# Time mixing: the substitution ahead of the strict scores, the queries behind the merges

## The chip, the cores and the metric

The kernel runs on one core of one Trainium2 chip. The metric is device microseconds (us) of one execution. Five engines work side by side, each through its own queue in a fixed order: TensorE (PE; its weight loads are listed as PEld), VectorE (DVE), ScalarE (ACT), GpSimd (POOL) and SyncE (SP, which only issues transfers here). An instruction that waits holds up everything behind it on its engine.

## The reference

The program runs two small transformer blocks of two layers each over 256 tokens of width 1024. The change lies in the first mixer, a recurrence over tokens with 16 heads of width 64:

```python
def _rwkv7_step(S, inp):
    r, w, k, v, a, b = inp
    sa = jnp.einsum('bhvk,bhk->bhv', S, a)
    S = S * w[:, :, None, :] + sa[..., None] * b[:, :, None, :] + v[..., None] * k[:, :, None, :]
    y = jnp.einsum('bhvk,bhk->bhv', S, r)
    return S, y
...
    y = jnp.moveaxis(y, 0, 1)
    mean = jnp.mean(y, axis=-1, keepdims=True)
    var = jnp.mean(jnp.square(y - mean), axis=-1, keepdims=True)
    yn = ((y - mean) * lax.rsqrt(var + LNX_EPS)).reshape(B, T, D) * lnx_w + lnx_b
    bonus = (jnp.sum(rh * kh * r_k, axis=-1, keepdims=True) * vh).reshape(B, T, D)
    out = ((yn + bonus) * g).astype(x.dtype)
    return out @ w_o
```

Seven more stages follow it (feed-forward, two kinds of attention and more); they take about 1130 of the 1420 us and their code isn't touched.

## The kernel before

**How the recurrence is computed.** It isn't stepped through. Tokens come in two blocks of 128 (b = 0, 1) and heads in two halves of eight (H = 0, 1). Within a block the recurrence is a triangular system for each head, I minus a strictly lower triangular matrix, and its inverse is built up by size: 16x16 blocks, then 32x32, then 64x64.

- `rwkv_base` (L1720 on) makes the small diagonal blocks on PE (L1745), masks them on DVE (L1747), and inverts all 16x16 blocks at once by forward substitution: for each row r from 2 to 15 one product (L1768) and one sum (L1769) on DVE, each needing the one before. Transposes and a copy (L1772 to L1774) put the result where the merges read it.
- `rwkv_strict` (L1839) computes the full 128x128 lower triangular scores for each H and b by `rwkv_scores`: PE at L1848 into a PSUM bank, DVE at L1850 from the bank with the mask. There are four such (H, b), each with two banks.
- `rwkv_merge` (L1783) joins blocks in four rounds of many tiny matmuls, which this text calls r1 to r4: r1 (L1791, 256 matmuls of 32x16) and its copy on DVE (L1792), r2 (L1798) and L1800 to L1804, r3 (L1811, which reads the strict scores) and L1818, r4 (L1824) and L1827. The copies L1827 fill Y64, the inverse of 64x64.
- `rwkv_solve` (L1854) makes the key scores (again L1848 and L1850, with other operands), sums them with the values (L1863), and applies Y64 in two halves (L1879 and its copy L1880, with L1874 and L1876 between). For b = 0 the state update L1887 and L1888 follows.
- `rwkv_gate` (L1917) projects the output gate on PE (L290 to L292 and L1925) and copies it on ACT (L1926). `rwkv_query` (L1928) multiplies the queries (L1934), transposes them on PE (L1702, copied at L1704 and L1705), makes the bonus sums (L1937 to L1940) and the bonus terms on POOL (L1943 to L1947).

The projections of key, value and query (`project`, 48 groups of L290 to L292 for each half of the columns) run in the background: `weave` steps its generators in turn and calls `tick`, which emits one step of the background list. Their weights are cut in two parts by the feeder at L88 (ACT) and L89 (DVE).

**What sets the order.** The code emits instructions in the order in which `weave` steps the generators. A scheduler then sorts each engine's queue, by what is ready in its own model of time and by the numbers given with `pri` or `high_priority`; a higher number goes first. `issue_after(ins)` ties all instructions that the block emits on the engine of `ins` behind `ins` in that engine's queue. PSUM has eight banks in rings: `tp` and `acc` have four each in this stage until L1586, where `tp` and `long` get four each.

Of the kernel before, what the change touches and what calls it, by code (L numbers as in the profile page):

```python
# [16 lines left out]
OP = mybir.AluOpType  # L17
# [131 lines left out]
class K:  # L149
# [1265 lines left out]
    def rwkv(self):  # L1415
        nc, W, A = self.nc, self.W, self.a
# [9 lines left out]
        for i in range(2):  # L1426
            c = slice(64 * i, 64 * i + 64)
# [15 lines left out]
        with self.tc.high_priority(1000):  # L1443
            for b in range(2):
# [4 lines left out]
                for g in range(2):  # L1449
                    p = self.tp()  # L1450
# [27 lines left out]
        raw = {}  # L1478
# [61 lines left out]
        E = [{"mv": self.sm(16, tag="mv", bufs=2)} for _ in range(2)]  # L1540
# [22 lines left out]
        xr = shifted(0, True)  # L1563
        self.bg.append(project("r", xr))
        self.weave([self.pri(1000, self.rwkv_keys(E[H], raw["k"][H])) for H in range(2)], n=1)
        self.weave([self.pri(200, self.rwkv_base(E))] + [self.pri(0, self.rwkv_strict(E[H])) for H in range(2)], n=1)
        while len(self.bg) > 1:
            self.tick()
        W.lo_pool = False
        gate = self.gate_parts(hid)  # L1570
        self.weave([self.pri(1000, self.rwkv_merge(E[H])) for H in range(2)] + [self.pri(400, self.rwkv_gate(H, E[H], *gate)) for H in range(0)], n=2)
        solve = ([self.pri(400, self.rwkv_solve(H, 0, E[H], raw["v"][H])) for H in range(2)]
                 + [self.pri(400, self.rwkv_gate(H, E[H], *gate)) for H in range(0, 2)])
        if 0:
            self.rings(2, 4, 2)
            self.weave(solve, n=0)
            solve = []
        self.drain()
        W.lo_pool = False
        W.cap = W.n_split  # L1580
        self.rings(0, 4, 4)
        vecs = [self.bcast(A[n][0].rearrange("h n -> (h n)") if n == "a_r_k" else A[n][0], D)
                for n in ("a_r_k", "a_lnx_w", "a_lnx_b")]
        self.weave(solve + [self.pri(400, self.rwkv_query(H, E[H], raw, vecs)) for H in range(2)])
        self.rope_setup()
        W.cap = len(W.plan)  # L1586
        W.grow(4)
# [195 lines left out]
    def rwkv_merge(self, E):  # L1783

        nc = self.nc
        Moff, P1z, Xv, Yc, Y32, Y64 = (E[n] for n in ("Moff", "P1z", "Xv", "Yc", "Y32", "Y64"))
        p1 = self.tp()
        for h in range(16):
            for i in range(4):
                s = slice(32 * i, 32 * i + 32)  # L1790
                nc.tensor.matmul(p1[s, h * 16:(h + 1) * 16], Moff[s, h, :], Xv[s, h, :], start=True, stop=True)  # L1791
        nc.vector.tensor_copy(P1z[:, :, :16], p1[:, :256].rearrange("p (h c) -> p h c", h=16))  # L1792
        yield
        pz = self.tp()
        for h in range(16):
            for i in range(4):
                s = slice(32 * i, 32 * i + 32)
                nc.tensor.matmul(pz[s, h * 16:(h + 1) * 16], P1z[s, h, :], Yc[s, h, :], start=True, stop=True)  # L1798
        nc.vector.tensor_scalar(Y32[:, :, :16], Yc, self.even, None, op0=OP.mult)
        nc.vector.scalar_tensor_tensor(Y32[:, :, 16:], Yc, self.odd, pz[:, :256].rearrange("p (h c) -> p h c", h=16),  # L1800
                                       op0=OP.mult, op1=OP.add)
        flat = lambda t: t.rearrange("p h c -> p (h c)")
        X32 = Moff
        nc.vector.transpose(flat(X32), flat(Y32))  # L1804
        yield
        p1 = self.tp()
        for h in range(16):
            b, hd = self.unhb(h)
            for i in (0, 64):
                s, t = slice(i, i + 32), slice(i + 32, i + 64)  # L1810
                nc.tensor.matmul(p1[t, h * 32:(h + 1) * 32], E["SM", b][s, hd, t], X32[s, h, :], start=True, stop=True)  # L1811
        P1 = P1z
        for i in (0, 64):
            s, t = slice(i, i + 32), slice(i + 32, i + 64)
            nc.gpsimd.memset(Y64[t, :, :32], 0.0)
            nc.scalar.activation(Y64[s, :, :32], Y32[s], AF.Copy)
            nc.scalar.activation(Y64[t, :, 32:], Y32[t], AF.Copy)
            nc.vector.tensor_copy(P1[t], p1[t].rearrange("p (h c) -> p h c", h=16))  # L1818
        yield
        pz = self.tp()  # L1820
        for h in range(16):
            for i in (0, 64):
                s, t = slice(i, i + 32), slice(i + 32, i + 64)
                nc.tensor.matmul(pz[s, h * 32:(h + 1) * 32], P1[t, h, :], Y32[t, h, :], start=True, stop=True)  # L1824
        for i in (0, 64):
            s = slice(i, i + 32)
            nc.vector.tensor_copy(Y64[s, :, 32:], pz[s].rearrange("p (h c) -> p h c", h=16))  # L1827
        yield

    @staticmethod  # L1830
# [98 lines left out]
    def rwkv_query(self, H, E, raw, vecs):  # L1929
        nc = self.nc  # L1930
        r_k, lnx_w, lnx_b = (self.vec_half(t, H) for t in vecs)
        heads = lambda t: t.rearrange("p b (h n) -> p (b h) n", h=8)
        R, V, EP = raw["r"][H], raw["v"][H], E["EP"]
        nc.vector.tensor_tensor(EP, R, EP, op=OP.mult)  # L1934
        E["R2"] = []
        yield from self.feat_pairs(EP, E["R2"])
        nc.gpsimd.tensor_tensor(R, E["Kt"], r_k, op=OP.mult)  # L1937
        nc.vector.tensor_tensor(R, EP, R, op=OP.mult)
        bon = self.sm(16)
        nc.vector.tensor_reduce(bon, heads(R), axis=AX.X, op=OP.add)  # L1940
        T2, G = R, E["G"]
        yield
        nc.gpsimd.tensor_tensor(heads(T2), heads(V), self.over_cols(E["mv"], 64), op=OP.add)  # L1943
        nc.gpsimd.tensor_tensor(heads(T2), heads(T2), self.over_cols(bon, 64), op=OP.mult)
        nc.gpsimd.tensor_tensor(T2, T2, lnx_b, op=OP.add)
        nc.gpsimd.tensor_tensor(T2, T2, G, op=OP.mult)
        nc.gpsimd.tensor_tensor(G, G, lnx_w, op=OP.mult)  # L1947
        E["T2"] = T2
# [122 lines left out]
```

## Time and profile before

| | |
|---|---|
| median of 3 runs | 1421.07 us (1416.91 to 1426.39) |
| profiled execution, its own time | 1423.76 us |
| its span | 1421.9 us |
| mean granted TensorE clock | 0.971 |
| busy share of the span: PE, DVE, ACT, POOL | 94%, 69%, 51%, 22% |
| the part of the stage that the change moves | about 94 to 191 us of the span |

The span lies 1.86 us under the execution's own time. A granted clock of 1.00 is 2.4 GHz, of 0.50 is 1.2 GHz. The busy shares are averages over eight stages; what the change is worth is read from its own stretch.

### The profile page before, as it was taken

The page shows a single profiled execution, that of the slowest core. Times are in us where ns is not written, and L with a number is a line of the kernel's source. Part 1 is how long each engine was busy: PE and PEld are TensorE (multiplying, and loading weights), DVE is VectorE, ACT ScalarE, POOL GpSimd, SP SyncE. Part 2 cuts the span into 40 slices and gives each one's busy share as a digit, 9 for nine tenths or more (in the row PEclk, how much of TensorE's full clock was granted, in tenths as well). Part 3 has the DMA queues.
Part 4 walks back from the last instruction along what each step waited for, and adds up shares of the span by engine and source line. Part 5 has one row for each costly group of instructions (what it writes and reads, how often), then busy time and mean ns, then how long its engine had stood idle before and what let it go on. Part 6 is the DMA issues. An engine that isn't in the chain of part 4 may idle for free. (4 is left out here: it accounts for less than half of the span.)

```text
span 1421.9 us, 20925 instructions
## 1 busy us (share of the span) xinstructions
PE 1339.9 (94%) x7819; PEld 1116.4 (79%) x7819; DVE 982.4 (69%) x1712; ACT 723.2 (51%) x1276; POOL 312.1 (22%) x278
## 2 busy tenths in 40 slices
PE   7998799989999799999999999999999998999998
PEld 5786699778888687788877777788888776788887
DVE  7889545788854675678864688677633897687642
ACT  5843212566643575576654555555543545465431
POOL 4201621100000100133222353222322631111110
PEclk9998599999999899999999999999999999999999
DMA  8345002466672452275574544265763632266662
GB/s 259 120 128 181 2 16 80 159 204 183 193 237 89 147 169 60 90 217 183 178 225 150 178 148 119 87 202 185 227 194 96 206 114 80 74 195 191 191 197 87
DMA packets 153574, 214.79 MB, mean 151 GB/s; under 512 B 11700, under 2 KB 95900, under 8 KB 153472
## 3 DMA queue, kind: packets, MB, share of 16 engines
q1 hardware_dynamic: 152608, 210.31, 47.6%
q10 hardware_dynamic: 864, 3.15, 0.6%
q8 instruction: 61, 1.00, 0.3%
q14 instruction: 41, 0.34, 0.1%
HBM read 212.37 MB, written 1.05 MB: 150 GB/s over the span
## 5 line engine op out<-in xcount | busy, mean ns | idle before, releaser
L88 ACT ACTIVATE s_slot<-s_slot 128x1024 fp32r<-128x1024 f32 (+2 forms) x221 | 229.6, 1045 | 166.8 <-PE bank L292 104.6
L89 DVE TENSOR_TENSOR s_slot<-s_slot,s_slot 128x1024 fp32r<-128x1024 f32 (+1 forms) x180 | 224.7, 1254 | 102.7 <-ACT s_slot L88 102.1
L89 DVE TENSOR_TENSOR rwkv_slot<-s_slot,rwkv_slot 128x1024 fp32r<-128x1024 f32 (+4 forms) x121 | 151.8, 1261 | 91.7 <-ACT rwkv_slot L88 91.2
L88 ACT ACTIVATE rwkv_slot<-s_slot 128x1024 fp32r<-128x1024 f32 (+3 forms) x141 | 144.7, 1034 | 88.3 <-PE bank L292 52.3
L89 POOL TENSOR_TENSOR s_slot<-s_slot,s_slot 128x1024 fp32r<-128x1024 f32 x41 | 100.9, 2460 | 303.0 <-ACT s_slot L88 283.0
L532 PE MATMUL bank<-ffn_slot,s_slot 128*128 128x512 f32 x320 | 115.2, 401 | 5.4 <-DVE ffn_slot L537 5.4
L532 PE MATMUL bank<-ffn_slot,rwkv_slot 128*128 128x512 f32 x280 | 98.4, 395 | 0.0
L532 PE MATMUL bank<-mlp_slot,s_slot 128*128 128x512 f32 x272 | 96.7, 396 | 0.6 <-DVE mlp_slot L537 0.6
L266 POOL TENSOR_TENSOR rwkv_sm<-rwkv_sm,mhalf 128x1 f32<-128x1 f32 x32 | 19.8, 618 | 340.0 <-DVE rwkv_sm L263 339.2
L534 PE MATMUL bank<-ffn_slot,s_slot 128*128 128x256 f32 x320 | 89.9, 281 | 0.0
L534 PE MATMUL bank<-ffn_slot,rwkv_slot 128*128 128x256 f32 x280 | 77.8, 278 | 0.0
L532 PEld LDWEIGHTS bank<-ffn_slot,s_slot 128*128 128x128 f32 x320 | 61.2, 191 | 20.8 <-DVE ffn_slot L537 6.4
L534 PE MATMUL bank<-mlp_slot,s_slot 128*128 128x256 f32 x272 | 75.8, 279 | 0.0
L89 POOL TENSOR_TENSOR rwkv_slot<-s_slot,rwkv_slot 128x1024 fp32r<-128x1024 f32 (+1 forms) x20 | 47.3, 2364 | 92.6 <-ACT rwkv_slot L88 75.1
L290 PE MATMUL bank<-s_slot,mlp_slot 128*128 128x512 f32 x160 | 62.6, 391 | 0.1
L292 PE MATMUL bank<-s_slot,mlp_slot 128*128 128x512 f32 x160 | 62.3, 390 | 0.0
L291 PE MATMUL bank<-s_slot,mlp_slot 128*128 128x512 f32 x160 | 62.3, 389 | 0.0
L532 PEld LDWEIGHTS bank<-ffn_slot,rwkv_slot 128*128 128x128 f32 x280 | 52.5, 188 | 12.4 <-DVE ffn_slot L537 0.3
L534 PEld LDWEIGHTS bank<-ffn_slot,s_slot 128*128 128x128 f32 x320 | 61.3, 192 | 0.0
L532 PEld LDWEIGHTS bank<-mlp_slot,s_slot 128*128 128x128 f32 x272 | 51.0, 188 | 12.8 <-DVE mlp_slot L537 0.9
L534 PEld LDWEIGHTS bank<-ffn_slot,rwkv_slot 128*128 128x128 f32 x280 | 52.6, 188 | 0.2
L532 PE MATMUL bank<-mlp_slot,rwkv_slot 128*128 128x512 f32 x144 | 51.7, 398 | 0.6 <-DVE mlp_slot L537 0.6
(514 smaller groups left out, 3549.4 us busy)
## 6 DMA issues: line engine op xcount, KB each, us to landing
s_slot<-in_mlp_w_dram SPq DMA_DIRECT2D x128, 512.0 KB, 4.4
s_slot<-in_ffn_w_in_dram SPq DMA_DIRECT2D x88, 512.0 KB, 4.2
s_slot<-in_ffn_w_out_dram SPq DMA_DIRECT2D x44, 512.0 KB, 4.2
s_slot<-in_a_w_rkv_dram SPq DMA_DIRECT2D x24, 512.0 KB, 4.4
s_slot<-in_diff_w_in_dram SPq DMA_DIRECT2D x32, 256.0 KB, 4.2
s_slot<-in_dsa_w_in_dram SPq DMA_DIRECT2D x16, 512.0 KB, 4.1
s_slot<-in_a_w_o_dram SPq DMA_DIRECT2D x8, 512.0 KB, 3.9
s_slot<-in_o_w_dram SPq DMA_DIRECT2D x8, 512.0 KB, 3.9
```

The lines of the kernel that those rows point to most:

```text
L88: k.nc.scalar.activation(hi, raw, AF.Copy)
L89: (k.nc.gpsimd if low else k.nc.vector).tensor_tensor(lo, raw, hi, op=OP.subtract)
L266: nc.gpsimd.tensor_tensor(r, u, self.mhalf[:, 0:1], op=OP.pow)
L290: mm(out, lh, rh, start=start, stop=False)
L291: mm(out, lh, rl, start=False, stop=False)
L292: mm(out, ll, rh, start=False, stop=stop)
L532: mm(o, wh[:, kt % 4, c], a.rearrange("p c t -> p (c t)"), start=kt == 0, stop=False, skip_group_check=True)
L534: mm(o[:, :T], wl[:, kt % 4, c], a[:, 0], start=False, stop=kt == 7, skip_group_check=True)
```

## The change

The substitution is woven alone, before any strict scores. The merges and the strict scores are then stepped together by hand: twice one step of both merges and two steps of each strict generator, and then the rest. The merges take their banks from the `acc` ring, since the strict scores hold those of `tp`. Solve, gate and query are emitted inside `issue_after` on the merges' last copy (L1827), which is a DVE instruction, so it is their DVE instructions that are tied. One product of the bonus sums (L1937) goes from POOL to DVE.

```diff
-        self.weave([self.pri(200, self.rwkv_base(E))] + [self.pri(0, self.rwkv_strict(E[H])) for H in range(2)], n=1)
+        self.weave([self.pri(1000, self.rwkv_base(E))], n=1)
         while len(self.bg) > 1:
             self.tick()
-        W.lo_pool = False
         gate = self.gate_parts(hid)
-        self.weave([self.pri(1000, self.rwkv_merge(E[H])) for H in range(2)] + [self.pri(400, self.rwkv_gate(H, E[H], *gate)) for H in range(0)], n=2)
-        solve = ([self.pri(400, self.rwkv_solve(H, 0, E[H], raw["v"][H])) for H in range(2)]
-                 + [self.pri(400, self.rwkv_gate(H, E[H], *gate)) for H in range(0, 2)])
...
+        merges = [self.pri(1000, self.rwkv_merge(E[H])) for H in range(2)]
+        strict = [self.pri(300, self.rwkv_strict(E[H])) for H in range(2)]
+        for _ in range(2):
+            for g in (*merges, *strict, *strict):
+                next(g, None)
+            self.tick(2)
+        self.weave([*strict, *merges], n=2)
         self.drain()
...
-        self.weave(solve + [self.pri(400, self.rwkv_query(H, E[H], raw, vecs)) for H in range(2)])
+        with ExitStack() as st:
+            for e in E:
+                st.enter_context(self.tc.issue_after(e["merged"].ins))
+            self.weave([self.pri(400, self.rwkv_solve(H, 0, E[H], raw["v"][H])) for H in range(2)]
+                       + [self.pri(400, self.rwkv_gate(H, E[H], *gate)) for H in range(2)]
+                       + [self.pri(400, self.rwkv_query(H, E[H], raw, vecs)) for H in range(2)])
@@ rwkv_merge
-        p1 = self.tp()
+        p1 = self.acc()
...
-            nc.vector.tensor_copy(Y64[s, :, 32:], pz[s].rearrange("p (h c) -> p h c", h=16))
+            E["merged"] = nc.vector.tensor_copy(Y64[s, :, 32:], pz[s].rearrange("p (h c) -> p h c", h=16))
@@ rwkv_query
-        nc.gpsimd.tensor_tensor(R, E["Kt"], r_k, op=OP.mult)
+        nc.vector.tensor_tensor(R, E["Kt"], r_k, op=OP.mult)
```

The lines of the changed kernel stand 3 higher in this stage: its L1853 is L1850 of before, its L1795 is L1792. The text keeps to the numbers of before.

First, DVE from the last sum of the substitution to the first copy of the merges. Before, the queue holds a key score (bank 67), three instructions of the bonus sums (L1938, L1940) and another key score ahead of the copy L1792:

```order
L1769 TENSOR_REDUCE rwkv_slot_794<-rwkv_slot_796 128x2x15
L1772 STREAM_TRANSPOSE rwkv_slot_796<-rwkv_slot_794 128x512
L1773 COPY rwkv_slot_794<-rwkv_slot_794 128x512
L1774 STREAM_TRANSPOSE rwkv_slot_796<-rwkv_slot_794 128x512
L1799 TENSOR_SCALAR rwkv_slot_1070<-rwkv_slot_796,even_odd 128x16x16 x2
L1850 TENSOR_TENSOR rwkv_slot_1508<-bank_67,rwkv_slot_97 128x512
L1938 TENSOR_TENSOR rwkv_slot_612<-rwkv_slot_503,rwkv_slot_612 128x1024
L1940 TENSOR_REDUCE rwkv_sm_496<-rwkv_slot_612 128x16
L1938 TENSOR_TENSOR rwkv_slot_613<-rwkv_slot_511,rwkv_slot_613 128x1024
L1850 TENSOR_TENSOR rwkv_slot_1512<-bank_68,rwkv_slot_97 128x512
L1792 COPY rwkv_slot_792<-bank_72 128x16x16
```

Now the strict scores stand there, four for b = 0 ahead of the transpose L1775 (L1772 of before) and four for b = 1 ahead of the copy, of which the first of each is shown:

```order
L1772 TENSOR_REDUCE rwkv_slot_794<-rwkv_slot_796 128x2x15
L1853 TENSOR_TENSOR rwkv_slot_1192<-bank_72,rwkv_slot_97 128x512
...
L1775 STREAM_TRANSPOSE rwkv_slot_796<-rwkv_slot_794 128x512
L1776 COPY rwkv_slot_794<-rwkv_slot_794 128x512
L1917 TENSOR_TENSOR rwkv_slot_1051<-rwkv_slot_1044,rwkv_slot_1051 32x1024
L1777 STREAM_TRANSPOSE rwkv_slot_796<-rwkv_slot_794 128x512
L1802 TENSOR_SCALAR rwkv_slot_1042<-rwkv_slot_796,even_odd 128x16x16 x2
L1853 TENSOR_TENSOR rwkv_slot_1340<-bank_72,rwkv_slot_97 128x512
...
L1795 COPY rwkv_slot_792<-bank_69 128x16x16
```

The eight strict scores went from inside the substitution to behind it, and the bonus sums and key scores from ahead of the copy to behind the merges.

Second, PE from the end of the query projection to the first matmul of r1. Before, half of the first key scores and the gate of b = 0 stand there:

```order
L292 MATMUL bank_68<-s_slot_89,rwkv_slot_599 128x512
L1848 MATMUL bank_67<-rwkv_slot_215,rwkv_slot_631 128x256 x2
L1848 MATMUL bank_68<-rwkv_slot_227,rwkv_slot_644 128x256 x2
L290 MATMUL bank_69<-rwkv_slot_1077,rwkv_slot_1080 128x512
...
L1925 MATMUL bank_70<-rwkv_slot_1079,rwkv_slot_1080 128x512
L1791 MATMUL bank_72<-rwkv_slot_796,rwkv_slot_793 32x16
```

Now the strict scores of b = 1 do, into banks that the strict scores of b = 0 hold until DVE has read them:

```order
L292 MATMUL bank_68<-s_slot_89,rwkv_slot_599 128x512
L1851 MATMUL bank_72<-rwkv_slot_218,rwkv_slot_734 128x256 x2
L1851 MATMUL bank_74<-rwkv_slot_218,rwkv_slot_734 128x256 x2
L1851 MATMUL bank_73<-rwkv_slot_230,rwkv_slot_745 128x256 x2
L1851 MATMUL bank_71<-rwkv_slot_230,rwkv_slot_745 128x256 x2
L1794 MATMUL bank_69<-rwkv_slot_796,rwkv_slot_793 32x16
```

The gate and all key scores went behind r4.

Third, DVE behind the merges in the changed kernel, from the last copy of r4 to the first copy of the solve; before, only four L1850 of `rwkv_solve` and the copies of the queries' transposes were left by then, between L1818 and L1880:

```order
L1830 COPY rwkv_slot_795<-bank_68 32x16x32
L1937 TENSOR_TENSOR rwkv_slot_503<-rwkv_slot_612,rwkv_slot_503 128x1024
...
L1940 TENSOR_TENSOR rwkv_slot_612<-rwkv_slot_506,rwkv_slot_1502 128x1024
L1853 TENSOR_TENSOR rwkv_slot_1508<-bank_67,rwkv_slot_97 128x512
...
L1941 TENSOR_TENSOR rwkv_slot_613<-rwkv_slot_511,rwkv_slot_613 128x1024
L1853 TENSOR_TENSOR rwkv_slot_1512<-bank_70,rwkv_slot_97 128x512
L1943 TENSOR_REDUCE rwkv_sm_496<-rwkv_slot_612 128x16
L1708 COPY rwkv_slot_1529<-bank_67 64x4x128
...
L1883 COPY rwkv_slot_1590<-bank_71 64x512
```

All of L1934 to L1940 and the four key scores, in turn, now stand between the merges and the solve.

## Rows read from the trace of the kernel before

**Rows 1.** Stretches of 4 us: length, busy us (instructions) by engine, granted clock, transfers.

```profile
128.00:132.00 4.00, 1.80 (x6) 0.91 (x6) 3.86 (x6) 1.88 (x2) 1.16 (x1) 0.94 1.02 273
...
148.00:152.00 4.00, 0.87 (x4) 0.71 (x4) 3.96 (x7) 0.00 (x0) 2.58 (x1) 0.50 0.00 0
...
172.00:176.00 4.00, 4.00 (x15) 3.21 (x15) 2.17 (x4) 0.00 (x0) 0.76 (x2) 0.51 0.00 0
...
188.00:192.00 4.00, 4.00 (x62) 3.93 (x60) 2.33 (x8) 2.47 (x3) 0.00 (x0) 1.00 0.02 4
```

**Rows 2.** The timeline of DVE during the substitution: start us, us, instructions.

```profile
106.01 0.68 DVE L1850 TENSOR_TENSOR rwkv_slot<-bank,rwkv_slot 128x512 f32<-128x512 f32 x1
106.61 1.21 DVE L89 TENSOR_TENSOR s_slot<-s_slot,s_slot 128x1024 fp32r<-128x1024 f32 x1
...
127.91 1.22 DVE L1934 TENSOR_TENSOR rwkv_slot<-rwkv_slot,rwkv_slot 128x1024 f32<-128x1024 f32 x1
129.06 0.35 DVE L1769 TENSOR_REDUCE rwkv_slot<-rwkv_slot 128x20 f32<-128x200 f32 x1
...
131.41 2.10 DVE L1768 TENSOR_TENSOR rwkv_slot<-rwkv_slot 128x288 f32<-128x288 f32 x1
133.54 0.45 DVE L1769 TENSOR_REDUCE rwkv_slot<-rwkv_slot 128x24 f32<-128x288 f32 x1
134.03 1.22 DVE L1914 TENSOR_TENSOR rwkv_slot<-rwkv_slot,rwkv_slot 32x1024 fp32r<-32x1024 f32 x1
...
138.36 0.62 DVE L1769 TENSOR_REDUCE rwkv_slot<-rwkv_slot 128x30 f32<-128x450 f32 x1
```

**Rows 3.** The timeline of PE from the projections to the merges' end.

```profile
109.64 2.86 PE L1848 MATMUL bank<-rwkv_slot,rwkv_slot 128*128 128x256 f32 x12
...
126.33 0.39 PE L291 MATMUL bank<-s_slot,rwkv_slot 128*128 128x512 f32 x1
126.55 0.39 PE L292 MATMUL bank<-s_slot,rwkv_slot 128*128 128x512 f32 x1
...
139.85 2.85 PE L1791 MATMUL bank<-rwkv_slot,rwkv_slot 32*32 32x16 f32 x194 [3.34 <-DVE rwkv_slot L1772]
...
144.23 1.09 PE L1791 MATMUL bank<-rwkv_slot,rwkv_slot 32*32 32x16 f32 x62 [1.53 <-issue]
...
152.18 2.77 PE L1798 MATMUL bank<-rwkv_slot,rwkv_slot 32*32 32x16 f32 x186
...
163.78 2.08 PE L1848 MATMUL bank<-rwkv_slot,rwkv_slot 128*128 128x256 f32 x4 [0.99 <-ACT rwkv_slot L1926]
...
165.79 0.31 PE L1824 MATMUL bank<-rwkv_slot,rwkv_slot 32*32 32x32 f32 x2
...
168.04 3.62 PE L1824 MATMUL bank<-rwkv_slot,rwkv_slot 32*32 32x32 f32 x126
```

**Rows 4.** The timeline of DVE and POOL beside the merges.

```profile
142.36 4.64 POOL L1937 TENSOR_TENSOR rwkv_slot<-rwkv_slot,rwkv_slot 128x1024 f32<-128x1024 f32 x2
...
144.74 3.35 DVE L1938 TENSOR_TENSOR rwkv_slot<-rwkv_slot,rwkv_slot 128x1024 f32<-128x1024 f32 x1 [1.71 <-POOL rwkv_slot L1937]
...
150.99 0.75 DVE L1792 COPY rwkv_slot<-bank 128x256 f32<-128x256 f32 x2
...
171.60 2.58 DVE L1827 COPY rwkv_slot<-bank 32x512 f32<-32x512 f32 x4 [2.77 <-PE bank L1824]
```

**Rows 5.** The timeline of PE behind the merges.

```profile
177.50 1.45 PE L1863 MATMUL bank<-rwkv_slot,rwkv_slot 128*128 128x64 f32 x12
...
187.05 2.02 PE L1874 MATMUL bank<-rwkv_slot,rwkv_slot 64*64 64x64 f32 x31
...
190.88 0.49 PE L1888 MATMUL bank<-rwkv_slot,rwkv_slot 128*128 128x128 f32 x2
```

**Rows 6.** Stretches of 1 us at the start of the next stage, columns as in Rows 1.

```profile
300.00:301.00 1.00, 0.57 (x1) 0.50 (x2) 1.00 (x5) 0.89 (x2) 0.00 (x0) 0.50 0.14 24
...
305.00:306.00 1.00, 1.00 (x6) 0.86 (x5) 0.63 (x2) 0.71 (x2) 0.00 (x0) 0.70 0.53 185
```

More of the change, by code (lines that the diff above doesn't have):

```diff
@@ L1565, in rwkv @@
         self.weave([self.pri(1000, self.rwkv_keys(E[H], raw["k"][H])) for H in range(2)], n=1)
-        self.weave([self.pri(200, self.rwkv_base(E))] + [self.pri(0, self.rwkv_strict(E[H])) for H in range(2)], n=1)
+        self.weave([self.pri(1000, self.rwkv_base(E))], n=1)
         while len(self.bg) > 1:
             self.tick()
-        W.lo_pool = False
         gate = self.gate_parts(hid)
-        self.weave([self.pri(1000, self.rwkv_merge(E[H])) for H in range(2)] + [self.pri(400, self.rwkv_gate(H, E[H], *gate)) for H in range(0)], n=2)
-        solve = ([self.pri(400, self.rwkv_solve(H, 0, E[H], raw["v"][H])) for H in range(2)]
-                 + [self.pri(400, self.rwkv_gate(H, E[H], *gate)) for H in range(0, 2)])
[L1574 to L1577, printed above, removed]
+        merges = [self.pri(1000, self.rwkv_merge(E[H])) for H in range(2)]
[5 more added lines that the diff above has]
+        self.weave([*strict, *merges], n=2)
         self.drain()
-        W.lo_pool = False
         W.cap = W.n_split
@@ L1793, in rwkv_merge @@
         yield
-        pz = self.tp()
+        pz = self.acc()
         for h in range(16):
@@ L1805, in rwkv_merge @@
         yield
-        p1 = self.tp()
+        p1 = self.acc()
         for h in range(16):
@@ L1819, in rwkv_merge @@
         yield
-        pz = self.tp()
+        pz = self.acc()
         for h in range(16):
```

## The prediction, made blind

> **What bounds the kernel now.** I read the windows first, because the page's shares are averages over eight stages. [Rows 1] is the place: from 128 us on PE falls to 0.87 busy us of 4, its granted clock goes from 1.00 to 0.50 (at 1.2 GHz instead of 2.4), and it is back only in the stretch that ends at 176. From there to the end of the stage PE is busy without a break (4.00 of 4 at 188). So the stage loses time in one hole, and what is won inside it should reach the end of the run, since the PE work behind it is the same and in the same order.
>
> Inside the hole I followed the timelines of PE and DVE. The query projection ends on PE at 126.94 (126.55 + 0.39) [rows 3]. DVE works through the substitution without idle time until 138.98 (138.36 + 0.62) [rows 2], and r1 starts at 139.85, behind the transpose L1772 [rows 3]. r1 ends at 145.32 (144.23 + 1.09), but r2 starts at 152.18 [rows 3]: the copy L1792 runs only at 150.99, because DVE's queue holds L1938 ahead of it, which waited for POOL's two products of L1937 and then ran 3.35 us, where its twin is a plain product of about 1.2 [rows 2, 4]. r4 starts at 165.79 and ends at 171.66 (168.04 + 3.62), with key scores between its matmuls [rows 3]. The work behind r4 is PE's alone: 171.66 to 190.88, where the state update L1888 begins [rows 3, 5]. I use that 190.88 as the mark: all that the change moves lies before it.
>
> **The change, part by part.**
>
> *End of the substitution.* Eight strict scores leave DVE's queue, each 0.60 us start to start (106.01 to 106.61), two L1934 at 1.15 (127.91 to 129.06) and L1914 at 1.22 [rows 2]: 4.8 + 2.3 + 1.2 = 8.3 us, so 138.98 becomes 130.7. One L1768 took 2.10 us, while the sums beside it took 0.35 to 0.62 [rows 2]; it ran while POOL had an instruction, and whether that meets it again is open: 1.6 us, so the end lies between 129.1 and 130.7. I take 130.0. The cuts L89 of the weights stay in the queue, and PE frees their buffers a little earlier than before, since half the strict scores leave its projection (16 of 32 matmul passes at 0.24 us, 2.86 / 12 [rows 3]: 3.8 us).
>
> *Start of r1.* This is a new wait. The strict scores of b = 1 now stand on PE ahead of r1 and need the banks of b = 0, which DVE reads only behind the substitution. The first bank is free at 130.0 + 0.65, and then 16 passes follow. At 2.4 GHz they would take 3.8 us; at 1.2 GHz a pass took 0.52 (2.08 / 4) [rows 3], so 8.3 us. PE has been idle since about 123 by then, and in the old hole, where it ran out of matmuls at 129, the clock fell before 132 [rows 1], so it starts at 1.2 GHz. At the next stage dense matmuls ran from 300.5 until the clock came back at about 305.4, that is 4.9 us [rows 6]. By that, 9.4 passes go slowly and 6.6 at 0.24: 4.9 + 1.6 = 6.5 us. r1 starts at 137.1 instead of 139.85: **-2.7**. The bounds (129.1 and 3.8 us; 130.7 and 8.3 us) give -6.3 to -0.2. DVE's transpose L1772 stands only 2.4 us of scores behind the substitution and is in time.
>
> *From r1 to r2.* Nothing but strict scores stands ahead of L1792 now, and they are done while r1 runs (5.5 us). The two copies take 0.75 [rows 4], and 0.35 for the way to PE: 1.1 us instead of 6.86 (145.32 to 152.18): **-5.8**. It can't be less than about 0.7, nor more than the old wait, since L1938 is gone from there.
>
> *r2 to r4.* No row changes up to r4's start. r4 runs unbroken: 128 x 3.62 / 126 = 3.7 us instead of 5.87: **-2.2**. So r4 ends at 171.66 - 2.7 - 5.8 - 2.2 = 161.0.
>
> *Behind r4: what comes back.* PE now has the gate of b = 0 and half of the key scores there, which it did in its idle time before, and eight more transposes L1702. From 161.0: eight gate matmuls at 1.2 GHz, 0.45 each (twice the 0.22 between 126.33 and 126.55 [rows 3]), 3.6 us; with 1.3 us of key scores that makes the 4.9 us to the faster clock. Then 13.5 passes of key scores at 0.24, 3.2. Then 32 passes of L1863 at 0.12 (1.45 / 12 [rows 5]), 3.9, and 16 transposes, taken at the same 0.12, 1.9. Then L1879 for both H, 2.0 (like L1874 [rows 5]), the gate of b = 1, 1.8, four more groups of scores, 3.8, L1874, 2.0, eight passes of L1863, 1.0, L1879, 2.0, and 0.1 for the first L1887. Sum 4.9 + 3.2 + 3.9 + 1.9 + 2.0 + 1.8 + 3.8 + 2.0 + 1.0 + 2.0 + 0.1 = 26.6, so the mark is reached at 187.6. Before, that part took 19.2: **+7.4**.
>
> *Does DVE keep up?* Its queue from L1827 (161.0 + 2.6 [rows 4]) on: six products at 1.15 and two sums of the same size, taken at 1.2, four key scores at 0.6, four copies L1705 at the 0.65 of an L1827 (2.58 / 4 [rows 4]) and a short conversion, 0.2: 6.9 + 2.4 + 2.4 + 2.6 + 0.2 = 14.5 us, so L1880 can start at 178.1. By the PE sum, L1879 of the second half ends at about 178, and PE has the second gate, L1887 and two score groups (some 3 us) before it needs L1880. DVE is just covered; if that cover is gone, each us of DVE counts. L1937 costs DVE 2.3 us here, which is in the sum, and spares it the wait for POOL. POOL's later steps L1943 to L1947 end later than before; what reads them is the output of the heads, far behind the mark. ACT has only the copies it had.
>
> At this place a rule speaks. The row shows that L1938 took 3.35 us beside POOL's L1937 [rows 4]. The Trainium skill ("GPSIMD Engine Reference", Key points) says that POOL shares its SBUF interfaces with VectorE and that they contend when a VectorE instruction has two SBUF inputs. By that, the six products behind the merges would suffer if POOL's L1943 met them; in the new queue POOL starts those only after the first L1940, when the products are done, so the sum would be the same but for a us, and the trace agrees that a plain product beside an idle POOL takes 1.22 [rows 2].
>
> Sum: -2.7 - 5.8 - 2.2 + 7.4 = **-3.3 us** at the mark (190.88 to 187.6). From there on the order is that of before, and PE is dense, so it stays -3.3.
>
> **The rivals.**
>
> *Faster: the clock stays up.* If the strict scores of b = 1 bring 2.4 GHz and the tiny matmuls hold it, r4 (3.7 us at 1.2 GHz [rows 3]) and r3, which has as many matmuls of the same size, lose half, -3.7, and the gate and key scores behind r4 start at full speed, -2.5: -9.5 in all, 1411.6 us. For it: 1.00 is held through L1874 and L1879, also small, at 188 [rows 1]. Against it: those stand between dense matmuls, while r1 to r4 have waits of 1 to 3 us between them, and 0.50 lasted through all of them before.
>
> *Slower: PE behind r4 stays at 1.2 GHz.* The key scores' banks are read by DVE in turn with the bonus sums, so PE gets its work there piecemeal: the last L1850 of the four ends at about 163.6 + 9.3 = 172.9. If these small waits keep the clock down until the transposes are through, the key scores cost 7.0 instead of 3.2 us and L1863 with the transposes 11.6 instead of 5.8: +9.6, so +6.3 net, 1427.4 us. It decides from about a third of that on: with more than 3.3 us of slow work behind the first 4.9 us the change is a loss. For it: the clock did not come back in the old hole while key scores alternated with waits, and only just before 176 [rows 1]. Against it: the eight gate matmuls and the key scores of both halves stand together and wait for little. The Trainium skill ("TensorE: Matmul & The Clock Gate", HAM oscillation) says just this of thin work with waits between: each pause costs the clock again. No run here shows which it is in the new queue.
>
> *No effect.* That the change doesn't move what it says is out: the order shows it. But if the substitution ends at 130.7 and the b = 1 scores run slow throughout, r1 is nearly where it was, and the sum is -0.8: 1420.3.
>
> **How the numbers follow.** The profiled execution took 1423.76 us, 2.7 over the median of the three runs (1421.07). 1423.76 - 3.3 = 1420.5 for such an execution, and 1421.07 - 3.3 = 1417.8 for a median: forecast 1418. Chances: the forecast within 3 us 0.62, the faster rival 0.16, the slower rival 0.17, no effect or something unseen 0.05. The range for 8 in 10 takes in most of both rivals and, since single runs of before spread by 5 us to each side, stays at 1410 to 1426. One per cent is 14.2 us, about what a measurement of this kernel can tell from no change. No case above reaches it; the clock held up everywhere together with the best r1 (-3.6 more) would come to -13. So faster by over 1% gets 0.05, slower 0.02, within 0.93.
>
> **What would show it.** In the changed profile: the last sum of the substitution ends at 129 to 131; r1 starts at about 137, behind L1848 at 1.2 GHz and not behind L1772; r2 follows r1 by about 1 us; r4 ends near 161; L1888 starts at 187 to 188. The prediction is wrong if L89 holds the substitution back, if r1 to r4 run at another clock, or if PE shows idle time in front of L1863 or L1874.

## The result and the profile after

The changed kernel takes 1436.12 us (median of 6 runs, 1429.51 to 1439.99), the kernel before, run beside it, 1423.69 us (6 runs, 1416.91 to 1428.38). The ratio is 1.0082, 95% interval 1.0058 to 1.0106: slower by 12.4 us, where 1418 was forecast. The profiled execution took 1439.99 us, its span is 1438.2 us, its mean granted clock 0.967. Lines behind L1588 have moved by 3 (L1888 is now L1891, L1880 is L1883, L1792 is L1795).

The timeline of PE in the changed kernel, to be read against [rows 3] and [rows 5]:

```profile
128.03 5.96 PE L1851 MATMUL bank<-rwkv_slot,rwkv_slot 128*128 128x256 f32 x16 [5.45 <-DVE rwkv_slot L1853]
133.92 2.16 PE L1794 MATMUL bank<-rwkv_slot,rwkv_slot 32*32 32x16 f32 x209
138.25 0.67 PE L1794 MATMUL bank<-rwkv_slot,rwkv_slot 32*32 32x16 f32 x47 [2.16 <-issue]
139.51 1.29 PE L1801 MATMUL bank<-rwkv_slot,rwkv_slot 32*32 32x16 f32 x80 [0.59 <-DVE rwkv_slot L1795]
...
153.80 3.62 PE L1827 MATMUL bank<-rwkv_slot,rwkv_slot 32*32 32x32 f32 x124 [0.42 <-DVE rwkv_slot L1821]
...
182.51 2.08 PE L1882 MATMUL bank<-rwkv_slot,rwkv_slot 64*64 64x64 f32 x32
194.99 0.80 PE L1891 MATMUL bank<-rwkv_slot,rwkv_slot 128*128 128x128 f32 x2 [10.40 <-DVE rwkv_slot L1883]
...
207.44 1.95 PE L1851 MATMUL bank<-rwkv_slot,rwkv_slot 128*128 128x256 f32 x8
```

Up to 184.59 (182.51 + 2.08) PE was ahead of the forecast. r1 starts at 133.92 instead of 139.85, r2 follows r1 by 0.59 us (138.92 to 139.51), r4 ends at 157.42 instead of 171.66, and PE has done all work ahead of the mark at 184.59, where it stood at 190.88 before. Then it does nothing for 10.40 us. The row of L1891 says what for: the copy L1883, on DVE. The windows show what the pause costs besides (columns as in [rows 1]):

```profile
156.00:160.00 4.00, 4.00 (x56) 3.42 (x53) 2.60 (x5) 0.00 (x0) 1.05 (x2) 0.51 0.02 4
160.00:164.00 4.00, 4.00 (x19) 3.22 (x17) 3.97 (x4) 1.09 (x2) 0.67 (x2) 1.00 0.00 0
...
188.00:192.00 4.00, 0.00 (x0) 0.00 (x0) 3.93 (x3) 0.00 (x0) 3.92 (x3) 0.50 0.00 0
...
196.00:200.00 4.00, 4.00 (x20) 4.00 (x20) 0.84 (x2) 0.00 (x0) 0.00 (x0) 0.50 0.00 0
```

The clock came back behind r4 (1.00 from 160 on). In the pause it fell again (0.50 from 188 on), and the block of L1891 runs at 0.50. The last block of key scores, L1851 x8, starts at 207.44. The kernel before has it at 200.54:

```profile
200.54 1.95 PE L1848 MATMUL bank<-rwkv_slot,rwkv_slot 128*128 128x256 f32 x8
```

4.1 us from the mark and 2.8 from the lower clock behind it make 6.9.

What does DVE do in those 10 us? Its timeline, and under it POOL's:

```profile
173.85 1.23 DVE L688 CAST rwkv_slot<-pos_i 128x2 f32<-128x2 int32 x1
...
175.84 1.28 DVE L1883 COPY rwkv_slot<-bank 64x512 f32<-64x512 f32 x2
177.04 0.17 DVE L692 TENSOR_TENSOR rwkv_slot<-rwkv_slot 128x32 f32<-128x32 f32 x1
177.14 1.27 DVE L1853 TENSOR_TENSOR rwkv_slot<-bank,rwkv_slot 128x512 f32<-128x512 f32 x2
178.34 1.13 DVE L693 TENSOR_TENSOR rwkv_slot<-rwkv_slot 128x16 f32<-128x16 f32 x1
179.50 1.84 DVE L700 TENSOR_SCALAR rwkv_slot<-rwkv_slot 128x48 f32<-128x48 f32 x1
181.26 2.38 DVE L703 COPY rwkv_slot<-rwkv_slot 128x48 f32<-128x48 f32 x1
183.57 2.38 DVE L701 TENSOR_SCALAR rwkv_slot<-rwkv_slot 128x48 f32<-128x48 f32 x1
185.98 2.26 DVE L702 TENSOR_SCALAR rwkv_slot<-rwkv_slot 128x48 f32<-128x48 f32 x1
188.28 4.95 DVE L705 SCALAR_TENSOR_TENSOR rwkv_slot<-rwkv_slot 128x48 f32<-128x48 f32 x3
193.26 0.19 DVE L706 TENSOR_SCALAR rwkv_slot<-rwkv_slot 128x48 f32<-128x48 f32 x1
...
194.24 1.30 DVE L1883 COPY rwkv_slot<-bank 64x512 f32<-64x512 f32 x2
```

```profile
177.08 2.36 POOL L1948 TENSOR_TENSOR rwkv_slot<-rwkv_slot,rwkv_slot 128x1024 f32<-128x1024 f32 x1
...
181.26 2.35 POOL L1949 TENSOR_TENSOR rwkv_slot<-rwkv_slot,rwkv_slot 128x1024 f32<-128x1024 f32 x1
183.56 2.35 POOL L1948 TENSOR_TENSOR rwkv_slot<-rwkv_slot,rwkv_slot 128x1024 f32<-128x1024 f32 x1
...
190.58 2.34 POOL L1950 TENSOR_TENSOR rwkv_slot<-rwkv_slot,rwkv_slot 128x1024 f32<-128x1024 f32 x1
```

L688 to L712 belong to `rope_setup`, called right behind the loop over solve, gate and query. It prepares sines and cosines of positions for a later attention stage: an iota and 24 fills on POOL (L686, L690), a short conversion (L688) and thirteen small steps (L692 to L712, on 16 to 48 numbers a partition) on DVE, two sines on ACT (L709, L713). PE has nothing to do with it. In the kernel before each DVE step takes 0.17 to 0.21 us, and POOL's last bonus term is done (187.10) before the first of the thirteen. DVE's timeline and POOL's there:

```profile
187.84 0.18 DVE L703 COPY rwkv_slot<-rwkv_slot 128x48 f32<-128x48 f32 x1
...
188.41 0.21 DVE L705 SCALAR_TENSOR_TENSOR rwkv_slot<-rwkv_slot 128x48 f32<-128x48 f32 x1
...
191.09 0.69 DVE L1880 COPY rwkv_slot<-bank 64x512 f32<-64x512 f32 x1
```

```profile
184.75 2.35 POOL L1947 TENSOR_TENSOR rwkv_slot<-rwkv_slot,rwkv_slot 128x1024 f32<-128x1024 f32 x1
```

In the changed kernel L703 takes 2.38 us (181.26 to 183.64) and ends 0.03 us after POOL's L1949 (183.61); L701 takes 2.38 and ends 0.04 us after POOL's L1948. The three L705 take 4.95 together. At 193.26, with POOL done (192.92), L706 takes 0.19 again. From L693 to the last L705, eight steps take 14.9 us instead of 1.6. The copy pair L1883 that PE waits for (194.24) stands behind all of them in DVE's queue.

Not every instruction suffers. L1853, which has one operand in PSUM, ran beside POOL's L1948 at 1.27 us for two (1.28 and 1.29 in the kernel before), and the first L1883 pair took 1.28 beside POOL's L1946. Nor do POOL's fills hold up a product: L1941 took 1.22 us at 165.83, while two fills (L1695, L1694) ran from 165.93 to 167.02.

**Behind 210 us** the first profile loses 9.4 us more against the kernel before (the same matmuls are 6.9 us late at 207 us and still at 299, at the end of the stage, and 16.3 at the end of the run), in code that the change doesn't touch. 3.0 us of it lie at one place, where the granted clock is 0.54 and the kernel before has 1.00: a matmul of L292 ahead of it is 10.2 us late (889.09 for 878.94), one behind it 13.2 (901.34 for 888.17).

```profile
896.00:901.00 5.00, 5.00 (x16) 3.87 (x16) 3.09 (x14) 2.05 (x10) 0.94 (x2) 0.54 0.00 0
```

### The profile page after: what moved, and what is told of

It is laid out like the page before. It is cut to its first block, busy times and chain, and to the rows that moved or that the text cites. A ratio compares the mean times of both kernels' runs of the same rounds, so it can differ in the third digit from the quotient of the medians.

```text
span 1438.2 us, 20939 instructions
## 1 busy us (share of the span) xinstructions
PE 1347.6 (94%) x7819; PEld 1125.4 (78%) x7819; DVE 997.1 (69%) x1714; ACT 724.4 (50%) x1276; POOL 305.1 (21%) x276
## 5 line engine op out<-in xcount | busy, mean ns | idle before, releaser
L292 PE MATMUL bank<-s_slot,mlp_slot 128*128 128x512 f32 x160 | 62.4, 390 | 0.0
```

Of the source, the lines that this page charges most:

```text
L292: mm(out, ll, rh, start=False, stop=stop)
```

## The experiments

Theory A was: a small DVE step on SBUF data waits for the POOL instruction that is running; the change pushed POOL's bonus terms later, beside `rope_setup`, and the steps of `rope_setup` ahead of a copy that PE needs. Rival B: DVE's queue behind the merges is simply too long now. Rival C: the loss lies in later stages. All ratios are against the kernel before, run on the same chip, with their 95% intervals.

**rope_late.** The call is written behind the next loop.

```diff
-        self.rope_setup()
         W.cap = len(W.plan)
...
+        self.rope_setup()
         self.rings(4, 2, 2)
```

> The changed kernel with one thing moved: the angles' set-up (rope_setup: the small VectorE steps L688 to L712 and the GpSimd fills L686 and L690) is written behind the second solve instead of in front of it. Theory A (each of these small VectorE steps waits for the GpSimd instruction that is running, and they stand ahead of the second pair of copies L1883, which PE waits for): the pair no longer waits, the first L1891 starts at 184.4 to 186 us instead of 194.99 and runs at a granted clock of 0.9 or more instead of 0.50, the last key score block L1851 x8 starts at 195 to 198 us instead of 207.44, and the time falls by 9 to 12 us, to 1424 to 1427. Rival B (the loss is the order behind the merges itself, with VectorE's queue too long by the products L1940): the first L1891 stays later than 190 us and the time above 1432. Rival C (the loss sits behind 210 us, in stages that the change does not touch): L1891 comes early as in A, and the time still stays above 1430.

1420.77 us (10 runs), ratio 0.9978 (0.9963 to 0.9993): 15.3 us under the changed kernel's median, and now faster than the kernel before. PE's timeline:

```profile
183.97 0.49 PE L1891 MATMUL bank<-rwkv_slot,rwkv_slot 128*128 128x128 f32 x2
...
193.62 1.95 PE L1851 MATMUL bank<-rwkv_slot,rwkv_slot 128*128 128x256 f32 x8
```

The pause is gone, and the last key scores start 13.8 us earlier than 207.44. That is 13.8 of the 15.3 us; the time came out better than expected, since I had reckoned with more of the loss behind 210 us. B and C are out as the main cause.

**rope_early.** The call is written ahead of the loop, just after `W.cap = W.n_split`.

> The changed kernel with the angles' set-up written ahead of solve, gate and query, so that its small VectorE steps stand beside the merges, where GpSimd's wide products do not run yet. Theory A: each small step takes about 0.2 us as in the kernel before, the merges end within 3 us of 157.4, the first L1891 starts at 184.5 to 188 us, and the time is 1423 to 1429. Rival B (VectorE's queue behind the merges is what is too long): L1891 stays later than 190 us and the time above 1432.

1420.32 us, ratio 0.9983 (0.9962 to 1.0003). The small steps now stand beside the merges, where POOL is idle; r4 ends at 158.74 (155.12 + 3.62) and L1891 starts at 185.82, with DVE's queue behind the merges as long as in the changed kernel but for `rope_setup`. That is 2.7 us under the expected range, as rope_late was under its own.

**before_rope_late**, the control: the same move in the kernel before.

> The kernel before with the angles' set-up behind the second solve, the same move as in rope_late. Theory A: there the small steps ran beside an idle GpSimd at 0.2 us each and stood in nobody's way, so the move is worth nothing: L1888 starts at 190 to 191 us and the time is within 2 us of the kernel before. Rival F (the set-up is a cost wherever it stands, by its 24 fills, its small steps or its two sines): the move gains 5 us or more here too.

1424.19 us, ratio 0.9997 (0.9976 to 1.0017). The set-up costs nothing by itself, so rival F is out. Its trace also shows how far the mark moves by the clock alone: PE's timeline there has

```profile
168.45 2.30 PE L1824 MATMUL bank<-rwkv_slot,rwkv_slot 32*32 32x32 f32 x126
...
187.98 0.49 PE L1888 MATMUL bank<-rwkv_slot,rwkv_slot 128*128 128x128 f32 x2
```

r4 is in part at the faster clock (granted 0.91 from 168 to 172 us), where [rows 3] has it at 1.2 GHz, and L1888 starts at 187.98 instead of 190.88, below the expected 190 to 191, with no gain in the median. A single trace's mark is good to some 3 us.

**terms_halved.** Is it the instruction that is running, or POOL's whole chain? Each of the ten bonus-term instructions is cut in two halves.

```diff
...
-        nc.gpsimd.tensor_tensor(T2, T2, lnx_b, op=OP.add)
...
+        for b in range(2):
+            nc.gpsimd.tensor_tensor(T2[:, b], T2[:, b], lnx_b[:, b], op=OP.add)
...
```

> The changed kernel with each of GpSimd's ten bonus-term instructions (L1946 to L1950) cut into two of half the width, the same work in 20 instructions. Theory A (a small VectorE step waits just for the end of the GpSimd instruction that is running): the steps L693 to L705 take at most 1.3 us each instead of up to 2.4, 10 of them some 11 us instead of 20, and the second pair of copies L1883, some of which now also stand ahead of the last small steps, comes 7 to 10 us earlier than 194.24; time 1425 to 1430. Rival D (the small steps wait for GpSimd's whole chain, or are slowed in proportion to its busy time): the steps still end only with that chain, at 192 us or later, and the time stays within 2 us of 1436.

1428.92 us, ratio 1.0037 (1.0017 to 1.0057). DVE's timeline, POOL's, and PE's:

```profile
181.95 1.30 DVE L703 COPY rwkv_slot<-rwkv_slot 128x48 f32<-128x48 f32 x1
...
186.95 3.65 DVE L705 SCALAR_TENSOR_TENSOR rwkv_slot<-rwkv_slot 128x48 f32<-128x48 f32 x3
190.64 1.17 DVE L706 TENSOR_SCALAR rwkv_slot<-rwkv_slot 128x48 f32<-128x48 f32 x1
191.84 0.86 DVE L1896 TENSOR_TENSOR rwkv_slot<-bank,rwkv_sm 64x256 f32<-64x256 f32 x2
```

```profile
184.37 2.50 POOL L1953 TENSOR_TENSOR rwkv_slot<-rwkv_slot,rwkv_slot 128x512 f32<-128x512 f32 x2
```

```profile
192.75 2.08 PE L1851 MATMUL bank<-rwkv_slot,rwkv_slot 128*128 128x256 f32 x4 [3.98 <-DVE rwkv_slot L1896]
```

With halves of 1.25 us no step takes more than 1.30, so a step waits for the end of one instruction; rival D is out. The copies L1883 came at 183.73 and 185.73 and L1891 at 184.48, but the last small steps then stood ahead of L1896 and PE waited 3.98 us there: a smaller wait at a later place.

**product_pool.** One part undone: the product of keys and bonus weights goes back to POOL.

```diff
-        nc.vector.tensor_tensor(R, E["Kt"], r_k, op=OP.mult)
+        nc.gpsimd.tensor_tensor(R, E["Kt"], r_k, op=OP.mult)
```

> The changed kernel with one part undone: the product L1940 (L1937 of the kernel before) goes back from VectorE to GpSimd, twice 2.4 us there instead of twice 1.2 us on VectorE. This also puts the second pair of copies L1883 ahead of the small steps L692 to L712 in VectorE's order. Theory A: the first L1891 starts at 184.5 to 188 us because nothing that waits for GpSimd stands ahead of the pair; the small steps then wait for GpSimd's later chain (it ends at 195 us or later) in between the score products L1853 at 196 to 210 us and take back part of the gain, 2 to 8 us; time 1425 to 1433. Rival B (a longer VectorE queue is the loss): the gain is the 2.4 us of the two products alone, time 1433 to 1435.

1425.97 us, ratio 1.0008 (0.9989 to 1.0028). L1891 starts at 187.29, in the expected range, since the queue has the copies first here. The run shows that wide steps wait as well. DVE's timeline and POOL's:

```profile
164.10 3.36 DVE L1941 TENSOR_TENSOR rwkv_slot<-rwkv_slot,rwkv_slot 128x1024 f32<-128x1024 f32 x1 [0.93 <-POOL rwkv_slot L1940]
```

```profile
160.85 5.52 POOL L1940 TENSOR_TENSOR rwkv_slot<-rwkv_slot,rwkv_slot 128x1024 f32<-128x1024 f32 x2 [25.49 <-issue]
```

L1941, 1.22 us alone, ends 1.09 us after POOL's L1940 (166.37). It repeats what [rows 4] showed for L1938. The small steps mostly fell behind POOL's end (L700 at 194.02: 0.19 us), so the wait of the later scores that I expected did not come. The time lies in the expected range all the same, 5.2 us over rope_late's. Its trace shows 3.3 of them ahead of L1891 (187.29 against 183.97), with both L1941 held up by POOL (the second took 2.65 us). The rest I can't tell from it (1420.84, the lowest of its ten runs).

**base_first** and **no_order** price parts of the change. In base_first the kernel before has the substitution written first, nothing else.

```diff
-        self.weave([self.pri(200, self.rwkv_base(E))] + [self.pri(0, self.rwkv_strict(E[H])) for H in range(2)], n=1)
+        self.weave([self.pri(1000, self.rwkv_base(E))], n=1)
+        self.weave([self.pri(0, self.rwkv_strict(E[H])) for H in range(2)], n=1)
```

> The kernel before with one part of the change alone: the substitution written ahead of the strict scores, which come behind it; merges, rings, products and order as before. Expected by the terms of the prediction: the substitution ends at 129 to 132 us instead of 135.6 and the merges start 2 to 6 us earlier; the gap between the first two rounds stays at 5 us or more, since queries and bonus sums still stand among the copies; the second L1888-type block (L1889 here) starts at 185 to 190 us. VectorE's order here has the small steps of the set-up between the two pairs of copies again; by theory A they cost as much as GpSimd still works then, 0 to 5 us. Time 1418 to 1426.

1423.85 us, ratio 1.0004 (0.9984 to 1.0024): nothing. The substitution ends at 136.94, not at 129 to 132, since the scheduler puts the strict scores and L1935 among its last steps all the same. r1 starts at 137.81; L1889 at 189.21.

no_order is rope_late with an empty list in place of `E` in the loop over `issue_after`.

> rope_late without the ordering of solve, gate and query behind the merges: VectorE's products L1937 and L1940 and sums L1941 and L1943 stand in the substitution and between the merges' copies L1795 and L1803 again. Expected by the prediction's term for the gap: two L1940, two L1941 and two L1943 lie between the copies of the first round and the second round's input, some 7 us, of which PE waits 5 to 7; the merges end at 161 to 167 us instead of 157; VectorE's queue behind them is 9.7 us shorter, so that the first L1891 starts 0 to 4 us later than rope_late's 183.97. Time 1420 to 1425. If the ordering is worth nothing, L1891 starts at 183 to 185 us and the time is within 2 us of rope_late's 1420.8.

1422.59 us, ratio 0.9990 (0.9972 to 1.0009). DVE's timeline between r1 and r2:

```profile
139.81 2.34 DVE L1940 TENSOR_TENSOR rwkv_slot<-rwkv_slot,rwkv_slot 128x1024 f32<-128x1024 f32 x2
142.08 0.74 DVE L1795 COPY rwkv_slot<-bank 128x256 f32<-128x256 f32 x2
142.75 2.34 DVE L1941 TENSOR_TENSOR rwkv_slot<-rwkv_slot,rwkv_slot 128x1024 f32<-128x1024 f32 x2
```

Only the two L1940 get ahead of the copies, so r2 waits 2.5 us (140.12 to 142.64) and not 5 to 7; r4 ends at 159.33, L1891 starts at 185.87. The ordering is worth 1.9 us at the mark and 1.8 us in the medians, whose intervals overlap.

**acc_undone**: rope_late with the merges' banks from `self.tp()` again.

> rope_late with one part undone: the merges take their banks from the transposes' ring again, as in the kernel before. The strict scores then share banks with the merges and VectorE's order puts half of them behind the first round. Expected: first merge round starts 0 to 3 us earlier or later than rope_late's 133.6, merges end within 4 us of 156.8, time within 3 us of rope_late's 1420.8. If the ring is what carries the gain, merges end at 163 us or later and the time is 1424 or more.

1420.35 us, ratio 0.9977 (0.9955 to 0.9999). The ring is not what carries the gain. The edit moved more than the banks: the gate of b = 0 stands ahead of r1 again, and L1891 starts at 186.20, 2.2 us behind rope_late's, with no loss in the median.

**after_again**: the changed kernel a second time.

> The changed kernel itself a second time, for what lies behind 210 us: its first profile runs 6.9 us behind the kernel before at 207 us and 16.3 us at the end, with granted clocks of 0.50 to 0.55 around 896 to 901 us that the kernel before does not have there. If this is a chance of one execution, the second profile stays 6.5 to 8.5 us behind from 210 us to the end and has no such fall at 896 us, and the span is 1428 to 1431 us. If it is a habit of the changed kernel, the same fall at the same place comes again and the span is 1434 or more. The first L1891 starts at 194 to 196 us in either case.

1434.16 us (5 runs), ratio 1.0081 (1.0048 to 1.0113). L1891 waits 10.37 us and starts at 196.74, 0.7 us behind the expected range. The fall of the clock near 896 us is not there (windows, same columns):

```profile
892.00:898.00 6.00, 5.89 (x33) 4.71 (x34) 4.72 (x20) 3.82 (x17) 0.93 (x2) 1.00 0.18 63
```

This execution is 8.3 us late at 210 us and 10.4 at the end, 2 us over the range that I had given for a chance. So the 3 us at 896 belong to one execution and not to the change. The 2 us that this one loses behind 210 us stay unplaced, and so do some 6 of the first profile's 9.4.

**terms_behind** and **terms_behind2** keep DVE's queue as it hurts and take POOL's terms away from beside it. The first ordered them behind L712 with `issue_after`:

> The changed kernel with VectorE's order kept where it hurts (all small steps L692 to L712 of the set-up ahead of the second pair of copies) and GpSimd's ten bonus-term instructions ordered behind the last small step, so that GpSimd runs none of them beside the small steps. Theory A (each small step waits for the GpSimd instruction that runs): the steps from L693 to L712 take 0.17 to 0.25 us each, the second pair of copies comes at 183 to 185 us instead of 194.24, the block behind it (L1894 here) starts at 184 to 186 us, GpSimd's terms then run from some 181 to 204 us, and the time is 1419 to 1425. Rival B (VectorE's order with the small steps ahead of the pair is the loss, whatever GpSimd does): the pair stays later than 190 us and the time above 1431.

1434.74 us, ratio 1.0085 (1.0055 to 1.0115). The edit didn't do what it was to do: the tie holds on one engine only, L712 is DVE's, and POOL ran its terms at 171.66 to 193.90 as ever. The small steps took up to 2.38 us again and the pair came at 195.21. It tells nothing between A and B. The second gives POOL something that needs the angles first:

```diff
+        self.rope_mark = nc.gpsimd.tensor_copy(box[:, 7, :48], box[:, 2, :48])
...
+        with self.tc.issue_after(self.rope_mark.ins):
+            for H in range(2):
+                self.rwkv_terms(E[H], raw["r"][H], raw["v"][H])
```

> What terms_behind meant to do and didn't (an ordering binds only instructions of one engine, so that GpSimd's terms still ran at 171.7 to 193.9 us): here GpSimd first copies the angles after VectorE's last small step but three (a new line L714, a true dependency), and its ten bonus terms are ordered behind that copy. VectorE's order is the one that hurts, all small steps ahead of the second pair of copies. Theory A (each small step waits for the GpSimd instruction that runs): L693 to L705 take 0.17 to 0.25 us each, the second pair of copies (L1887 here) comes at 183 to 186 us, the block behind it starts at 184 to 187 us, and the time is 1418 to 1424. Rival B (VectorE's order is the loss, whatever GpSimd does): the pair stays later than 190 us and the time above 1431.

1420.00 us (12 runs), ratio 0.9979 (0.9959 to 0.9999). DVE's timeline, POOL's, and PE's:

```profile
176.94 0.18 DVE L703 COPY rwkv_slot<-rwkv_slot 128x48 f32<-128x48 f32 x1
...
177.97 0.69 DVE L705 SCALAR_TENSOR_TENSOR rwkv_slot<-rwkv_slot 128x48 f32<-128x48 f32 x3
...
183.55 0.69 DVE L1887 COPY rwkv_slot<-bank 64x512 f32<-64x512 f32 x1 [1.28 <-PE bank L1886]
```

```profile
182.52 3.76 POOL L1954 TENSOR_TENSOR rwkv_slot<-rwkv_slot,rwkv_sm 128x1024 f32<-128x1024 f32 x2
```

```profile
184.38 0.49 PE L1895 MATMUL bank<-rwkv_slot,rwkv_slot 128*128 128x128 f32 x2
```

The same thirteen steps stand ahead of the same pair, and cost nothing: 0.18 us for L703, 0.69 for three L705. This is the cleanest of the runs: B is out, and A is shown. POOL's terms end at 203.87, 11 us later than in the changed kernel, and nobody waits for them.

**gate_in_merges**, a candidate: rope_late with the gate woven among the merges.

```diff
-        self.weave([*strict, *merges], n=2)
+        self.weave([*strict, *merges, *[self.pri(400, self.rwkv_gate(H, E[H], *gate)) for H in range(2)]], n=2)
...
-                       + [self.pri(400, self.rwkv_gate(H, E[H], *gate)) for H in range(2)]
```

> A candidate: rope_late with the gate's four products (14 wide instructions of PE per half, some 1.4 to 2.5 us a block) written beside the merges instead of behind them, where PE idles between rounds (0.6 to 2 us a gap) and its clock is granted at 0.50 at times. If the gaps take them, the merges end at 157 to 160 us, what is behind them has 5 to 6 us less for PE, the block L1891 starts at 180 to 183 us (rope_late 183.97), and the time is 1417 to 1420. If they lengthen the chain of rounds by as much as they save behind it, L1891 stays at 184 to 186 us and the time within 2 us of rope_late's 1420.8.

1424.62 us (12 runs), ratio 1.0018 (0.9995 to 1.0042): worse than rope_late. Behind r4 the wide gate matmuls are missing, and the clock is back only from 168 to 172 us and then from 188 on. Its windows, and rope_late's:

```profile
160.00:164.00 4.00, 2.04 (x8) 1.54 (x7) 3.88 (x6) 0.00 (x0) 2.44 (x5) 0.50 0.00 0
...
176.00:180.00 4.00, 4.00 (x24) 3.67 (x24) 1.48 (x2) 0.66 (x2) 3.92 (x3) 0.50 0.00 0
```

```profile
160.00:164.00 4.00, 3.76 (x19) 2.99 (x18) 3.97 (x5) 0.89 (x2) 1.04 (x2) 1.00 0.00 0
...
176.00:180.00 4.00, 4.00 (x46) 3.39 (x44) 1.21 (x2) 1.18 (x2) 4.00 (x3) 1.00 0.00 0
```

The key scores and the solve run at 1.2 GHz for most of their time, and the block of the state update starts at 192.94 instead of 183.97, later than in either case of the expectation. This is the course that the prediction's slower rival described. None of the traces with the whole gate behind r4 reads so low for so long (product_pool has 0.71 and 0.86 from 168 to 176 us); why the clock stays down here, no run shows.

## Why the prediction was wrong

The forecast was -3.3 us, the result +12.4. By its own steps:

- *End of the substitution*: 130.0 forecast, 127.37 measured (126.75 + 0.62). The meeting with POOL left open there did not take place.
- *Start of r1*: 137.1 forecast, 133.92 measured. The new wait for the banks of b = 0 is there, and the strict scores of b = 1 took 5.96 us at a rising clock, 6.5 forecast.
- *r1 to r2*: 1.1 forecast, 0.59 measured. *r4's end*: 161.0 forecast, 157.42 measured; r4 itself, with two short waits inside, took 5.0 us (152.47 to 157.42), not 3.7.
- *Behind r4*: 26.6 us of PE work forecast, 27.2 measured (157.42 to 184.59). The slower rival's clock did not stay down: PE's waits there were 0.2 to 0.3 us each, and the granted clock read 1.00 from 160 us on. A small misreading in the working: the mean of 0.70 from 305 to 306 us [rows 6] puts the return of the clock at about 305.6, not 305.4, which is worth some 0.1 us.
- *Does DVE keep up?* is the step that failed. It listed DVE's queue up to the first L1880 (178.1, "just covered") with "a short conversion, 0.2" for L688 (it took 1.23), and stopped there. The second pair, on which L1888 waits, stands behind thirteen small steps (L692 to L712), of which the kernel before has eight ahead of its last copy, at 0.2 us each. At that price they are 2.6 us, and PE would have waited for little or nothing. Eight of them took 14.9 because of the sentence two lines further on: "POOL's later steps L1943 to L1947 end later than before; what reads them is the output of the heads, far behind the mark." The data is read far behind; that the engine was busy is what counted. POOL's chain ended at 192.92 instead of 187.10, and began only at 170.64, so that it covered just the time in which `rope_setup` ran. Idle time of PE was among the prediction's signs of being wrong, in front of L1863 or L1874; it came in front of L1888.
- The rule was at hand, and was applied to too few instructions. "GPSIMD Engine Reference", Key points, in the Trainium skill names VectorE instructions with two SBUF inputs and those in a two-port mode; the prediction weighed it for the six wide products alone. This case's traces agree for two SBUF inputs: L1941 took 3.36 us. L703 and L701 have one and waited as well (2.38); in which mode they ran, no trace shows. A step with a PSUM operand (L1853) and the sum L1943 (1.22 us at 171.87, while POOL's L1946 ran until 172.54) weren't touched. A row of the kernel before was at hand too: L1768 took 2.10 us beside a POOL instruction [rows 2], and the prediction asked only whether that one step would meet POOL again.

Without that one collision the time would have come out near the forecast: rope_late, terms_behind2 and acc_undone lie 2.9, 4.0 and 4.0 us under the kernel before by their medians, where the sum said 3.3. That it is so near is in part luck: at the mark their traces are 6.9, 6.5 and 4.7 us ahead of 190.88 (183.97, 184.38 and 186.20), more than the sum said and more than the medians show, and a single trace's mark is good to some 3 us. The chances had little room for what happened: a loss of 0.8% is within one per cent, which had 0.93, but 1436.12 lies 10 us above the range of 1410 to 1426, "no effect or something unseen" had 0.05, and no rival had POOL in it. Three kernels here beat the kernel before with the whole of their intervals, by some 0.2%: rope_late, acc_undone and terms_behind2.

What stays open: some 2 us of the loss behind 210 us (6 in the first profile), and some 2 of the 5 us between product_pool and rope_late.

## What to carry to other kernels

When work moves on one engine, list everything that stays behind in the queues up to each instruction that the bound engine waits for, the unrelated small steps as well, and price each beside what the other engines will be running then. In these runs a DVE step of 0.2 us on SBUF data cost as much as the rest of the wide POOL instruction that it met, up to 2.4 us, so a chain of such steps beside a chain of wide POOL instructions advances by one step for each of them. Where such a chain can't move, keep POOL's wide work behind it by a true dependency, or put the copies that matter ahead.

## What the runs showed of the hardware

- The DVE step ends with the running POOL instruction if it is small (0.03 to 0.04 us behind it), and 1.09 us behind it if it is a wide product that takes 1.22 alone: 2.38 us for 48 numbers a partition beside instructions of 2.35, at most 1.30 beside halves of 1.25.
- POOL is held up as well. In the kernel before its L1943 took 2.81 us at 149.42, just behind the start of DVE's L1938 (149.26), and 1.90 the second time, at 154.17.
- The granted clock behind r4, by trace: with the whole gate behind r4 it read 0.95 or more from 164 to 168 us in all nine traces; in gate_in_merges, without it, 0.50 from 160 to 164, 0.69 to 168, and again 0.50 from 176 to 184, with PE busy 4.00 of 4 us there; in acc_undone, with the gate of b = 0 ahead of r1, 0.50 from 160 to 168.
